# The two score tiles of an attention head in one PSUM bank

## The chip, the core and the metric

The kernel runs on one core of a Trainium2 chip. A core has a matrix engine (TensorE, PE in the rows; its weight loads are PEld), a vector engine (VectorE, DVE), a scalar engine (ScalarE, ACT), GpSimd (POOL) and SyncE (SP), which issues most of the DMAs. Each engine works through its own instructions in the order of the program and waits on semaphores for the others. Matrix products land in PSUM, which has eight banks of 512 float32 values in each of 128 partitions; VectorE and ScalarE read them from there. The metric is the device time of one launch, in microseconds (us), as the median of a few runs.

## The reference

One layer of a streaming encoder, in float32, for 256 prompt rows and 32 rows of a running stream (288 columns in the kernel, which keeps everything transposed): a SwiGLU block, a mixing block with two branches (causal pooling, and latent attention with 16 heads), an output projection, a second SwiGLU block and a last RMSNorm. What matters here is the attention of the prompt rows. With `CHUNK = 64` and blocks of 128 queries it is, for each head:

```python
s = (jnp.einsum('bqhd,bshd->bhqs', qn, k_nope)
     + jnp.einsum('bqhr,bsr->bhqs', qr, k_rope)).astype(jnp.float32) * SM_SCALE
mask = k_chunk[None, :] <= (qp // CHUNK)[:, None]
s = jnp.where(mask[None, None], s, NEG_INF)
p = jax.nn.softmax(s, axis=-1).astype(v.dtype)
return jnp.einsum('bhqs,bshd->bqhd', p, v)
```

The mask lets queries 0 to 63 see 64 keys, 64 to 127 see 128, 128 to 191 see 192 and 192 to 255 see all 256.

## The kernel before, in words

**Weights.** All large products run over weight pieces that are read once. SP loads a piece into a raw buffer, ScalarE rounds it to the high part `whi` (line 185), VectorE subtracts to get the low part `wlo` (line 186), and TensorE forms the product in three passes (high by high, low by high, high by low; lines 151 to 153). Lists of steps are written out by the program and run in that order by `run()` (line 88); before a step's own work come the splits for the steps ahead of it, and what a step leaves for VectorE and ScalarE (its "post") is issued one step later (`later`, line 85). In the attention part a split is cut in two pieces of 512 columns. The schedule is manual: the order of the program is the order on every engine.

**PSUM.** Every product goes to a tile from one pool of eight buffers of one bank each (`acc()`, line 65). A buffer is handed out again when the last reader of its tile is done, and TensorE waits for that at the first product into the new tile.

**Attention.** The loop over heads (line 759) issues for head `hd`: the transposes of the probabilities of head `hd - 1` (`transposes`, line 632), the scores and the softmax of head `hd` (`scores`, line 618), after every fourth head the scores of the running stream for four heads together (`scores4`, line 657), the projections of the next pair of heads as filling work (`fill`, line 751: `q_rope`, `q_nope`, `k_nope`, `values`), the attended values of head `hd - 1` (`attend`, line 641, whose result leaves PSUM at lines 650 and 651), and now and then `spread4` (line 686), which takes the running stream's result of four heads out of one tile, 32 columns at a time, by ScalarE at line 691 and VectorE at line 692.

**Scores of a head.** Two tiles are taken from the pool. `outs[0]` holds queries 0 to 127 by keys 0 to 127 and is made with two float32 products (lines 620, 621). `outs[1]` holds queries 128 to 255 by keys 0 to 255 and is made with five products of split operands (lines 623 to 627). Then `softmax` (line 599) cuts each tile in its upper and lower 64 rows, which gives four pieces with 64, 128, 192 and 256 keys. It issues, in this order: four maxima on VectorE (line 610), four exponentials with a running sum on ScalarE (line 612), one reciprocal on VectorE (line 613) and two scalings of the probabilities on VectorE (line 615). The four maxima of a head stand ahead of its four exponentials in the program. The lines around them:

```python
for _, s, m, _ in seen:
    dve.tensor_reduce(out=m, in_=s, axis=AX.X, op=ALU.max, negate=True)
for p, s, m, t in seen:
    act.activation(p, s, AF.Exp, bias=m, accum_out=t)
```

The functions that the change touches, with the line numbers of the profile:

Of the kernel before, what the change touches and what calls it, by code (L numbers as in the profile page):

```python
# [14 lines left out]
P = 128  # L15
# [30 lines left out]
def kernel(ctx: ExitStack, tc: tile.TileContext, i, o):  # L46
# [18 lines left out]
    def acc():  # L65
        return psa.tile([P, 512], F32, tag="acc", name="acc")
# [532 lines left out]
    def softmax(parts):  # L599

        n = len(parts)
        nb = sm.tile([P, 2], F32, tag="nb", name="nb")
        su = sm.tile([P, 2], F32, tag="su", name="su")
        rs = sm.tile([P, 2], F32, tag="rs", name="rs")
        seen = []
        for b, (p, s, low, high) in enumerate(parts):
            rows = ((0, P, low),) if low == high else ((0, 64, low), (64, P, high))
            seen += [(p[r0:r1, :nk], s[r0:r1, :nk], nb[r0:r1, b : b + 1], su[r0:r1, b : b + 1]) for r0, r1, nk in rows]
# [4 lines that stand above are left out]
        dve.reciprocal(rs[:, :n], su[:, :n])  # L613
        for b, (p, _, _, _) in enumerate(parts):
            dve.tensor_scalar_mul(out=p, in0=p, scalar1=rs[:, b : b + 1])


    def scores(hd):
        outs = (acc()[:, :P], acc()[:, : 2 * P])
        pe.matmul(outs[0], qn[hd][:, :P], kn[hd][:, :P], start=True, stop=False)  # L620
        pe.matmul(outs[0], qr[hd // 2][:, :P], krz[hd % 2][:, :P], start=False, stop=True)
        q, k, r = qns.pop(hd), kns.pop(hd), qrs[hd // 2]
        pe.matmul(outs[1], q[:, 0, :], k[:, 0, :], start=True, stop=False)
        pe.matmul(outs[1], q[:, 0, :], k[:, 1, :], start=False, stop=False)
        pe.matmul(outs[1], q[:, 1, :], k[:, 0, :], start=False, stop=False)
        pe.matmul(outs[1], r[:, hd % 2, :], krh, start=False, stop=False)
        pe.matmul(outs[1], r[:, hd % 2, :], krl[hd % 2], start=False, stop=True)
        p = prompt_p[hd % 2]
        softmax([(p[b], outs[b], b * P + 64, b * P + P) for b in range(2)])
        pr[hd] = p  # L630
# [128 lines left out]
    for hd in range(HEADS + 1):  # L759
        old, four = hd - 1, hd and hd % 4 == 0  # L760
        if hd:
            step(lambda old=old: transposes(old))
        if four:
            step(transposes4)
        if hd < HEADS:
            step(lambda hd=hd: scores(hd))
            if hd % 4 == 3:
                step(lambda hd=hd: scores4(hd // 4))
            fill(hd, 0)
            if hd > 4 and hd % 4 == 1:  # L770
                step(lambda hd=hd: spread4(hd // 4 - 1))
        else:
            wo_parts((3, 0, 0), (3, 0, 1))
        if hd:
            step(lambda old=old: attend(old))
        if four:
            step(lambda old=old: attend4(old // 4))
        if hd < HEADS:
            fill(hd, 1)
        else:  # L780
            wo_parts((0, 1, 0))
            step(lambda old=old: spread4(old // 4))
# [143 lines left out]
```

## Time and profile before

| | |
|---|---|
| median of three runs | 2449.61 us (2449.33 to 2449.8) |
| profiled execution | 2448.82 us, its span 2447.1 us |
| TensorE, products | busy 2423.5 us, 99% of the span |
| TensorE, weight loads | busy 2415.1 us, 99% |
| VectorE | busy 1384.3 us, 57% |
| ScalarE | busy 993.2 us, 41% |
| GpSimd | busy 55.7 us, 2% |
| share of 16 DMA engines | 50.8% in the main queue |

All times in rows are us from the start of the span; a mean is in ns. A busy TensorE is not TensorE at its peak, since products overlap in it and their ends are modelled. The idle time of an engine is put down to the instruction that released it; where two instructions on one engine overlap in the rows, no idle time is shown between them. A number after an x is a count of instructions, and a row of a timeline with x2 or x4 stands for as many instructions in succession, with the name and shape of the first. Attention takes the stretch from about 1217 to 1400 us; the softmax of the first head starts at 1236.8 us.

### The profile page before, as it was taken

How to read it: one execution, taken by the hardware profiler on the slowest of the kernel's cores; microseconds unless marked ns; L12 is line 12 of the kernel's file. 1: busy time of each engine (PE TensorE's matmuls, PEld its weight loads, DVE VectorE, ACT ScalarE, POOL GpSimd, SP SyncE). 2: the span in 40 equal slices, each digit the busy share in tenths (PEclk: the TensorE clock that was granted, in tenths of full speed). 3: DMA queues.
4: the chain of work that ended last, by engine and by line, in shares of the span. 5: the costliest groups of instructions: out<-in, count | busy, mean ns of one | idle time of the engine just before them, and what ended most of it. 6: DMA issues, size and time to landing. Idle time of an engine off the chain costs nothing.

```text
span 2447.1 us, 43880 instructions
## 1 busy us (share of the span) xinstructions
PE 2423.5 (99%) x18298; PEld 2415.1 (99%) x18298; DVE 1384.3 (57%) x2056; ACT 993.2 (41%) x1472; POOL 55.7 (2%) x94
## 2 busy tenths in 40 slices
PE   9999999999999999999999999999999999999998
PEld 9999999999999999999999999999999999999997
DVE  7555555555555776544466675655555555555555
ACT  6333333333333535433367633433333333333334
POOL 0000000000000150000000000000000000000000
PEclk9999999999999999999999999999999999999999
DMA  7556446545644745544422365554554464455444
GB/s 236 174 148 187 164 147 181 173 162 148 189 162 149 221 154 171 185 164 164 155 97 86 113 197 181 162 168 162 148 186 164 147 189 164 158 153 189 164 143 129
DMA packets 129014, 399.71 MB, mean 163 GB/s; under 512 B 16160, under 2 KB 21536, under 8 KB 128816
## 3 DMA queue, kind: packets, MB, share of 16 engines
q1 hardware_dynamic: 126592, 392.73, 50.8%
q8 instruction: 143, 2.34, 0.4%
q0 software_dynamic: 1504, 3.15, 0.4%
q10 hardware_dynamic: 720, 1.04, 0.1%
q14 instruction: 55, 0.45, 0.1%
HBM read 391.35 MB, written 5.51 MB: 162 GB/s over the span
## 4 chain that ended last, share of the span: by engine, by line
PE 60%; issue 35%; ACT 3%; DVE 2%; DMA 0%; POOLq 0%; POOL 0%; ACTq 0%; DVEq 0%
PE acc L152 20%; PE acc L153 20%; PE acc L151 20%; ACT p L612 1%; ACT whi L185 1%; DVE wlo L186 1%; ACT sw L433 0%; DVE nb L610 0%; DVE y L822 0%; ACT kn L564 0%; ACT qrs L185 0%; DVE qn L550 0%; PE acc L225 0%; DVE kns L186 0%; DVE qr L436 0%
## 5 line engine op out<-in xcount | busy, mean ns | idle before, releaser
L186 DVE TENSOR_TENSOR wlo<-raw,whi 128x1024 fp32r<-128x1024 f32 (+2 forms) x858 | 919.4, 1075 | 667.7 <-ACT whi L185 664.0
L185 ACT CAST whi<-raw 128x1024 fp32r<-128x1024 f32 (+2 forms) x858 | 789.7, 925 | 918.4 <-PE acc L152 755.2
L151 PE MATMUL acc<-xh,whi 128*128 128x288 f32 x3600 | 1062.5, 295 | 5.4 <-ACT whi L185 5.4
L152 PE MATMUL acc<-xl,whi 128*128 128x288 f32 x3600 | 1064.1, 296 | 0.0
L153 PE MATMUL acc<-xh,wlo 128*128 128x288 f32 x3600 | 1062.8, 295 | 0.0
L151 PEld LDWEIGHTS acc<-xh,whi 128*128 128x128 f32 x3600 | 678.0, 188 | 5.4 <-ACT whi L185 5.4
L152 PEld LDWEIGHTS acc<-xl,whi 128*128 128x128 f32 x3600 | 678.3, 188 | 0.0
L153 PEld LDWEIGHTS acc<-xh,wlo 128*128 128x128 f32 x3600 | 677.6, 188 | 0.2 <-DVE wlo L186 0.2
L153 PE MATMUL acc<-mh,wlo 128*128 128x288 f32 x1408 | 415.0, 295 | 0.0
L152 PE MATMUL acc<-ml,whi 128*128 128x288 f32 x1408 | 415.0, 295 | 0.0
L151 PE MATMUL acc<-mh,whi 128*128 128x288 f32 x1408 | 414.3, 294 | 0.0
L152 PEld LDWEIGHTS acc<-ml,whi 128*128 128x128 f32 x1408 | 264.7, 188 | 0.0
L151 PEld LDWEIGHTS acc<-mh,whi 128*128 128x128 f32 x1408 | 264.6, 188 | 0.0
L153 PEld LDWEIGHTS acc<-mh,wlo 128*128 128x128 f32 x1408 | 264.6, 188 | 0.0
L277 ACT ACTIVATE s<-z 128x288 f32<-128x288 f32 x88 | 39.0, 445 | 233.4 <-DVE z L275 233.4
L275 DVE TENSOR_TENSOR z<-acc,r 128x288 f32<-128x288 f32 x88 | 40.2, 458 | 88.8 <-PE acc L153 84.7
L281 DVE TENSOR_TENSOR u<-acc,r 128x288 f32<-128x288 f32 x88 | 40.2, 457 | 84.8 <-PE acc L153 84.8
L151 PE MATMUL acc<-oh,whi 128*128 128x288 f32 x256 | 76.1, 297 | 0.5 <-DVE ol L692 0.5
L151 PE MATMUL acc<-mgh,whi 128*128 128x288 f32 x256 | 75.6, 295 | 0.0
L152 PE MATMUL acc<-mgl,whi 128*128 128x288 f32 x256 | 75.5, 295 | 0.0
L152 PE MATMUL acc<-ol,whi 128*128 128x288 f32 x256 | 75.5, 295 | 0.0
L153 PE MATMUL acc<-mgh,wlo 128*128 128x288 f32 x256 | 75.5, 295 | 0.0
(196 smaller groups left out, 1796.5 us busy)
## 6 DMA issues: line engine op xcount, KB each, us to landing
raw<-in_wg SPq DMA_DIRECT2D x172, 512.0 KB, 3.3
raw<-in_wu SPq DMA_DIRECT2D x172, 512.0 KB, 3.3
raw<-in_wd SPq DMA_DIRECT2D x128, 384.0 KB, 3.3
raw<-in_wd SPq DMA_DIRECT2D x128, 320.0 KB, 3.0
raw<-in_wga SPq DMA_DIRECT2D x32, 512.0 KB, 3.3
raw<-in_wgb SPq DMA_DIRECT2D x32, 512.0 KB, 3.3
raw<-in_wo SPq DMA_DIRECT2D x32, 512.0 KB, 3.3
raw<-in_wout SPq DMA_DIRECT2D x32, 512.0 KB, 3.3
```

Of the source, the lines that this page charges most:

```text
L151: pe.matmul(out, hi[:, c], xh, start=first, stop=False)
L152: pe.matmul(out, hi[:, c], xl, start=False, stop=False)
L153: pe.matmul(out, lo[:, c], xh, start=False, stop=last)
L185: act.copy(hi, src)
L186: dve.tensor_tensor(out=lo, in0=src, in1=f(hi), op=ALU.subtract)
L275: dve.tensor_tensor(out=z, in0=ps[:, :T], in1=st["r"], op=ALU.mult)
L277: act.activation(sv[m], z, AF.Silu)
L281: dve.tensor_tensor(out=u, in0=ps[:, :T], in1=st["r"], op=ALU.mult)
L612: act.activation(p, s, AF.Exp, bias=m, accum_out=t)
```

## The change

Instead of one tile for each of the two score blocks, one tile is taken from the pool, and the two blocks are columns 0 to 127 and 128 to 383 of it. A head so takes one PSUM buffer less. The products, the maxima, the exponentials and all shapes stay as they are, and so does their order in the program.

```diff
     def scores(hd):
-        outs = (acc()[:, :P], acc()[:, : 2 * P])
+        both = acc()
+        outs = (both[:, :P], both[:, P : 3 * P])
         pe.matmul(outs[0], qn[hd][:, :P], kn[hd][:, :P], start=True, stop=False)
         pe.matmul(outs[0], qr[hd // 2][:, :P], krz[hd % 2][:, :P], start=False, stop=True)
```

## Rows read from the trace of the kernel before

**Rows 1.** Busy time by stretch: from and to, length, then busy time and count of PE, PEld, DVE, ACT and POOL, the granted TensorE clock (1.00 is full), the DMA share and GB/s. First a stretch of the gate projections ahead of attention, then the stretch from the first softmax to the transposes of head 14.

```profile
1190.00:1210.00 20.00, 20.00 (x154) 20.00 (x152) 9.19 (x10) 7.66 (x11) 0.00 (x0) 1.00 0.48 153
1237.00:1386.40 149.40, 143.19 (x1085) 136.52 (x1083) 101.90 (x280) 106.60 (x328) 0.00 (x0) 1.00 0.28 93
```

**Rows 2.** Who waited for whom between 1225 and 1400 us, PE's own list, its two longest: engine, tile and line that waited, who released it, us in total, times, the longest.

```profile
PE acc L661 <- DVE ol L651: 3.5, 3, 1.4
PE acc L623 <- DVE ol L651: 1.2, 3, 0.4
```

**Rows 3.** The same list for DVE, its two longest and its last; every line left out has ACT as its releaser.

```profile
DVE rs L613 <- ACT p L612: 22.4, 16, 2.5
DVE wlo L186 <- ACT whi L185: 7.3, 17, 2.4
...
DVE nb L610 <- PE acc L621: 0.7, 1, 0.7
```

**Rows 4.** The same list for ACT, whole.

```profile
ACT p L612 <- DVE nb L610: 13.1, 15, 1.3
ACT qns L185 <- DVE qn L550: 12.5, 16, 1.2
ACT qrs L185 <- DVE qr L436: 12.0, 8, 1.5
ACT s L612 <- DVE nb L610: 4.7, 4, 1.2
ACT oh L691 <- DVE ol L692: 3.1, 9, 0.5
ACT pts L639 <- PE acc L637: 1.7, 1, 1.7
ACT vs L591 <- PE acc L583: 1.7, 1, 1.7
ACT L612 <- DVE nb L610: 0.7, 1, 0.7
```

**Rows 5.** All instructions of line 610 in the trace: count, shortest, median and longest in ns, first and last start, and how many of each shape (a head has one of each of the four).

```profile
L610 DVE TENSOR_REDUCE nb<-acc x68: 206/325/428, 1236.8 to 1391.6; 64x1 f32<-64x64 f32 x16, 64x1 f32<-64x128 f32 x16, 64x1 f32<-64x192 f32 x16, 64x1 f32<-64x256 f32 x16
```

**Rows 6.** Timeline of DVE over the softmax of head 7: start, length, engine, line, operation, tiles, shape, count, and the idle time before it with its releaser. The maxima stand in two rows of two, because the answer was cut between the second and the third.

```profile
1312.06 0.51 DVE L610 TENSOR_REDUCE nb<-acc 64x1 f32<-64x64 f32 x2
...
1312.60 0.79 DVE L610 TENSOR_REDUCE nb<-acc 64x1 f32<-64x192 f32 x2
1314.72 0.17 DVE L613 RECIPROCAL rs<-su 128x2 f32<-128x2 f32 x1 [1.32 <-ACT p L612]
```

**Rows 7.** Timeline of ACT over the same softmax: its first exponential and the end of its last one.

```profile
1312.69 0.31 ACT L612 ACTIVATE p<-acc,nb 64x64 f32<-64x64 f32 x1 [1.23 <-DVE nb L610]
...
1314.50 0.19 ACT L612 ACTIVATION_READ_ACCUMULATOR p<-acc,nb 64x1 f32 x1
```

**Rows 8.** The third maximum of the same head in the list by line and shape: busy us, mean ns, idle before.

```profile
L610 DVE TENSOR_REDUCE nb<-acc 64x1 f32<-64x192 f32 x1 | 0.3, 350 | 0.0
```

**Rows 9.** Timeline of ACT in one `spread4`, where ACT and DVE read one PSUM tile in turns, 32 columns each time: the second and the third block.

```profile
1337.98 0.18 ACT L691 CAST oh<-acc 128x32 fp32r<-128x32 f32 x1 [0.52 <-DVE ol L692]
1338.42 0.18 ACT L691 CAST oh<-acc 128x32 fp32r<-128x32 f32 x1 [0.26 <-DVE ol L692]
```

**Rows 10.** Timeline of DVE in the same `spread4`: the first and the second block.

```profile
1337.76 0.18 DVE L692 TENSOR_TENSOR ol<-acc,oh 128x32 fp32r<-128x32 f32 x1
1338.20 0.19 DVE L692 TENSOR_TENSOR ol<-acc,oh 128x32 fp32r<-128x32 f32 x1 [0.25 <-ACT oh L691]
```

**Rows 11.** Timeline of PE in the scores of head 0: the last products into the first and into the second score tile.

```profile
1236.37 0.39 PE L621 MATMUL acc<-krz,qr 128*128 128x128 f32 x2
...
1237.08 0.28 PE L627 MATMUL acc<-krl,qrs 128*128 128x256 f32 x1
```

**Rows 12.** Timeline of DVE in head 0: its four maxima.

```profile
1236.80 1.39 DVE L610 TENSOR_REDUCE nb<-acc 64x1 f32<-64x64 f32 x4 [0.69 <-PE acc L621]
```

**Rows 13.** Timeline of ACT in head 0: the copy of the last value block ahead of it, the load of the exponential's table, and the first exponential.

```profile
1236.35 0.37 ACT L591 COPY vs<-acc 128x256 f32<-128x256 f32 x1 [1.71 <-PE acc L583]
1237.40 1.28 ACT L612 ACT_TABLE_LOAD   x1 [0.68 <-DVE nb L610]
1238.70 0.31 ACT L612 ACTIVATE p<-acc,nb 64x64 f32<-64x64 f32 x1
```

**Rows 14.** Timeline of PE in the scores of head 8: the last product into the second score tile.

```profile
1319.15 0.28 PE L627 MATMUL acc<-krl,qrs 128*128 128x256 f32 x1
```

**Rows 15.** Timeline of DVE in head 8: its first two maxima.

```profile
1319.71 0.51 DVE L610 TENSOR_REDUCE nb<-acc 64x1 f32<-64x64 f32 x2
```

**Rows 16.** Timeline of PE around the transposes of head 14: the last product ahead of them, and the first transpose.

```profile
1385.60 0.29 PE L153 MATMUL acc<-oh,wlo 128*128 128x288 f32 x1
1386.46 0.30 PE L635 MATMUL acc<-ident,p 128*128 128x128 f32 x1 [0.58 <-ACT whi L185]
```

**Rows 17.** Timeline of DVE at the same place: the scalings of the probabilities of head 14.

```profile
1386.03 0.55 DVE L615 TENSOR_SCALAR p<-p,rs 128x128 f32<-128x128 f32 x2
```

**Rows 18.** Timeline of DVE at the end of the softmax of head 15.

```profile
1391.02 0.55 DVE L615 TENSOR_SCALAR p<-p,rs 128x128 f32<-128x128 f32 x2
```

**Rows 19.** Timeline of ACT after the transposes of head 15: the copy of their result.

```profile
1396.50 0.48 ACT L639 COPY pts<-acc 128x384 f32<-128x384 f32 x1 [1.72 <-PE acc L637]
```

**Rows 20.** Timeline of PE at the transposes of head 15.

```profile
1395.92 0.27 PE L635 MATMUL acc<-ident,p 128*128 128x128 f32 x1
```

## The prediction

> **What bounds the kernel now.** The page's first part names TensorE at 99%, and over the whole kernel that is right. The change acts in attention alone, so the view to read next is the busy time by stretch: in the gate projections TensorE is busy for 20.00 of 20.00 us, but from the first softmax to the transposes of head 14 for 143.19 of 149.40 us [rows 1]. There it stands still for 6.2 us, with the clock granted in full.
>
> The list of waits says for what. TensorE's two longest are line 661 (three times, 3.5 us) and line 623 (three times, 1.2 us), both released by VectorE's line 651 [rows 2]. Both are first products into a new PSUM buffer, and line 651 is the last reader of an older one: TensorE has run out of buffers. This is what one buffer less per head bears on.
>
> But a wait for a buffer is a wait for its reader, and the question is what the readers wait for. The lists of VectorE and ScalarE answer it: they wait for each other all through the stage, and for TensorE three times in it, at the first softmax (0.7), at the last value block before that (1.7), and once for 1.7 at line 639, which is after head 15 [rows 3, 4, 13, 19]. So from head 0 on, the chain of VectorE and ScalarE instructions sets the pace, and TensorE is ahead of it by as many buffers as it has. At the end of the stretch the chain catches it: the last product before the transposes of head 14 starts at 1385.60, and the first transpose at 1386.46 after 0.58 us of idleness [rows 16]. The releaser named there is a cast, but the transpose reads the probabilities, whose scalings run from 1386.03 [rows 17]. From that point on TensorE works without a pause worth naming, so what counts is when these scalings are done.
>
> **What the change removes.** Each head takes one buffer less, and TensorE can run further ahead. Counting buffers in the order in which the program frees them, line 661 would then wait for a tile freed long before, and the first product of `k_nope` in an odd head (line 151) would get the one that line 651 frees. The wait moves. I cost this at nothing: readers that never wait for TensorE do not get earlier because TensorE does, and the transposes of head 14 still wait for their probabilities. If that cover were gone, the gain would be bounded by the 6.2 us above (last rival).
>
> **What the change adds: an order between the two engines that read.** In `softmax` four maxima (VectorE) stand ahead of four exponentials (ScalarE), sixteen times in the trace [rows 5]. The exponential needs only its own piece's maximum. Yet in head 7 the first one starts at 1312.69 [rows 7]; the first two maxima run from 1312.06 and are done at 1312.06 + 0.51 = 1312.57, and the other two run from 1312.60 [rows 6]. So it waits for the second maximum, which reads the other 64 rows of the same tile, and not for the third, which reads the other tile. The same shows in `spread4`: ScalarE's second block starts at 1337.98 [rows 9], when VectorE's first block (1337.76 + 0.18 = 1337.94) is done [rows 10], though they read different columns and share only the PSUM tile. Two engines read one tile in turns, in the order of the program, whichever part each of them reads.
>
> With both blocks in one tile, the first exponential therefore waits for all four maxima. These are done at 1312.60 + 0.79 = 1313.39 [rows 6] instead of 1312.57: 0.82 us later. The other three exponentials stand behind it on ScalarE, and behind them the casts and copies of the fillers; on VectorE the reciprocal waits for the last exponential already (1.32 us in this head, 22.4 us in sixteen [rows 3, 6]) and comes 0.82 us later too. Both engines leave the softmax shifted by the same amount. ScalarE has no spare time there that could take it: it waits for the maxima in every head (15 times, 13.1 us, and once at the table load [rows 4]), so it is there early and starts late.
>
> The Trainium skill has the reason in "PSUM — Partial Sum Buffer", section "PSUM bank collisions raise a hardware error": two engines must not touch one bank in the same 32 partitions at once, two reads included. The trace agrees that reads take turns [rows 9, 10]. The page's rule is by 32 partitions, while the first exponential also waits for a maximum of other rows [rows 6, 7]; by the rule alone the wait would be shorter, which is the first rival below.
>
> Lower end for this term: nothing (an ordering that knows columns). Upper end: 0.82 plus another hand-over; from the end of the second maximum to the exponential lie 0.12 us now [rows 6, 7], so 0.94. I take 0.82, since the hand-over is there already.
>
> **The maxima wait for the last product.** VectorE's first maximum now waits for the second block's last product as well. Only head 0 feels this: there VectorE waits for TensorE. The first block is done at 1236.37 + 0.39 = 1236.76 and the second at 1237.08 + 0.28 = 1237.36 [rows 11], so the maxima start 0.60 later. The tightest of the later heads, head 8, has its last product done at 1319.15 + 0.28 = 1319.43 [rows 14] and its first maximum at 1319.71 [rows 15]: 0.28 us to spare, and both of them come later together.
>
> Head 0 in all: maxima from 1237.40 for 1.35 us (1.39 less a wait of 0.04 inside them, an estimate) end at 1238.75. The table load began 0.08 after the second maximum (1237.32, from 1236.80 + 0.51 by head 7's pair) [rows 6, 12, 13]; it would begin at 1238.83 instead of 1237.40. So head 0 adds 1.43 us.
>
> **The sum.** The probabilities of head 14 are later by head 0 and fourteen others: 1.43 + 14 × 0.82 = 12.9 us. TensorE waits for them now, so it is later by the same 12.9. Head 15 adds nothing more: its scalings start at 1391.02 [rows 18], its transposes at 1395.92 [rows 20], and 0.82 fits into that gap of 4.9. The other stages keep their order. The profiled execution took 2448.82, which gives 2461.7; the median of the runs lies 0.79 above the profiled one, and on it the time is 2449.61 + 12.9 = 2462.5.
>
> **Rivals.**
>
> *The order is kept by rows.* The first exponential (rows 0 to 63) waits for the third maximum (same rows) and the second for the fourth. The third takes 0.35 us [rows 8] and ends at 1312.95: 0.38 later than now; the second exponential would be held 0.02 more, since it can't start before 1313.39 + 0.12. Some 0.40 a head, and 1.0 in head 0: 1.0 + 14 × 0.40 = 6.6, so 2456.2. For it: the page's rule. Against it: the first exponential's wait for a maximum of other rows. Chance 0.09.
>
> *No new wait between the readers.* Disjoint columns of one tile are read side by side, so that the change does only what its words say. Then head 0's 0.6 is left: 2450.2. Against it stand the turns in `spread4`. Chance 0.05.
>
> *The freed buffer decides.* TensorE's pauses for buffers go and the stage runs at TensorE's pace: at most 6.2 us of standstill [rows 1] are won, 2443.4. It would take a chain that waits for TensorE somewhere, so that an earlier product makes an earlier reader, and by more than 0.82 us a head. For it speaks that TensorE's longest pauses are for buffers [rows 2]; against it that the readers wait for TensorE nowhere between head 0 and head 14 [rows 3, 4]. Chance 0.04.
>
> *More than the sum.* TensorE's pauses grow from 6.2 to some 19 us in the stretch. At today's pauses of up to 1.4 us the granted clock stays full [rows 1, 2]; should it fall to the lower of its two levels after longer ones, products there would take longer, past 2465. Chance 0.02.
>
> **How the numbers follow.** The forecast as worked out has 0.80. Its own range is 2460 to 2464.5: 0.12 more a head (the upper end above) adds 1.8, and a little slack somewhere takes off as much. The range to hold the time 8 times in 10 also takes in the order by rows, with as much below it: 2455.5 to 2465. What a measurement of this kernel can tell from no change is 0.2%, 4.9 us. Slower by more: the forecast, the order by rows and the last case, 0.91. Within: 0.05. Faster: 0.04.
>
> **What would show it.** In the changed kernel ScalarE's waits for line 610 rise from 13.1 to about 25 us, and VectorE's at line 613 from 22.4 to about 36; the first exponential starts 0.12 after the fourth maximum in every head. The time from the maxima of head 1 to the scalings of head 14 grows by 0.82 a head. TensorE's waits on line 661 go, and others grow: line 151 in odd heads, line 623 for the split keys. Wrong it would be if the first exponential still starts after the second maximum, if the chain waits for TensorE where it doesn't now, or if the shift is there but TensorE doesn't stand waiting at the transposes of head 14.

## The result, and the profile after

The changed kernel takes 2463.07 us (median of six runs, 2462.96 to 2463.6), against 2449.57 (2449.23 to 2449.8) for the kernel before, measured beside it: 13.5 us more. The ratio is 1.0056, with a 95% interval of 1.0045 to 1.0067. The profiled execution took 2463.41 us with a span of 2461.6. The source has one line more inside `scores`, so each number below that is higher by one: 620 is now 621, 651 is 652. In the experiments the numbers shift again with the lines that are put in; the names of the tiles tell what is meant (`nb` a maximum, `p<-acc` an exponential, `acc<-ident,p` a transpose).

The stretch from the first softmax to the transposes of head 14, which answers to [rows 1], has grown from 149.4 to 162.4 us:

```profile
1237.00:1399.40 162.40, 147.09 (x1085) 136.91 (x1083) 102.09 (x280) 107.03 (x328) 0.00 (x0) 1.00 0.26 86
```

The counts of instructions are those of before, and VectorE and ScalarE are busy for the same time within 0.5 us. They have not worked more, they have stood still more. TensorE's busy time has risen by 3.9 us with the same 1085 products. Single products are some 0.3 us long in the rows [rows 14, 16], but 1085 of them took 143.19 us before [rows 1], 0.13 each: they overlap, so that a pause can lie in part under the end of the product ahead of it, and the length of the stretch is the safer number. The granted clock is still 1.00.

Who waited between 1225 and 1412 us, VectorE's list and then ScalarE's (answers to [rows 3, 4]):

```profile
DVE rs L613 <- ACT p L612: 35.9, 16, 3.4
DVE sw L434 <- ACT sw L433: 6.8, 8, 0.9
...
DVE nb L610 <- PE acc L628: 1.3, 1, 1.3
```

```profile
ACT p L612 <- DVE nb L610: 25.2, 15, 2.1
ACT qns L185 <- DVE qn L550: 12.5, 16, 1.2
...
ACT L612 <- DVE nb L610: 2.1, 1, 2.1
ACT vs L591 <- PE acc L583: 1.7, 1, 1.7
ACT pts L640 <- PE acc L638: 0.8, 1, 0.8
```

Two waits have grown by much, both inside the softmax: ScalarE for the maxima from 13.1 to 25.2, VectorE at the reciprocal from 22.4 to 35.9. With them go head 0's two, for the first maximum (0.7 to 1.3) and at the table load (0.7 to 2.1). The others, as `qns`, are within 1.1 us of what they were. The softmax of head 7, VectorE and then ScalarE (answers to [rows 6, 7]):

```profile
1318.46 0.51 DVE L610 TENSOR_REDUCE nb<-acc 64x1 f32<-64x64 f32 x2
...
1318.98 0.79 DVE L610 TENSOR_REDUCE nb<-acc 64x1 f32<-64x192 f32 x2
1321.93 0.17 DVE L613 RECIPROCAL rs<-su 128x2 f32<-128x2 f32 x1 [2.15 <-ACT p L612]
```

```profile
1319.89 0.31 ACT L612 ACTIVATE p<-acc,nb 64x64 f32<-64x64 f32 x1 [2.03 <-DVE nb L610]
```

The four maxima are done at 1318.98 + 0.79 = 1319.77, and the first exponential starts 0.12 us after that. Before, it started 0.12 after the second. The idle times in brackets are longer by 0.80 and 0.83.

All exponentials of line 612 (count; shortest, median and longest in ns; first and last start) and the semaphore waits that stand at that line on ScalarE, first in the kernel before, then in the changed one:

```profile
L612 ACT ACTIVATE p<-acc,nb x64: 308/389/470, 1238.7 to 1390.2; 64x64 f32<-64x64 f32 x16, 64x128 f32<-64x128 f32 x16, 64x192 f32<-64x192 f32 x16, 64x256 f32<-64x256 f32 x16
L612 ACTq EVENT_SEMAPHORE  x32: 17/38/38, 1237.4 to 1389.5; - x32
```

```profile
L612 ACT ACTIVATE p<-acc,nb x64: 310/392/472, 1240.2 to 1404.1; 64x64 f32<-64x64 f32 x16, 64x128 f32<-64x128 f32 x16, 64x192 f32<-64x192 f32 x16, 64x256 f32<-64x256 f32 x16
L612 ACTq EVENT_SEMAPHORE  x16: 17/38/38, 1238.8 to 1402.5; - x16
```

The reads are as long as they were: 389 ns against 392 at the median, and the maxima 325 in both kernels [rows 5]. What has changed is the semaphores, on which one engine waits for another: two waits a head have become one. Before, the second and the fourth maximum of a head raise a semaphore; now only the fourth does. So the order is kept by waits of the program, and no slower read shows.

The last pause of the stage, at the transposes of head 14, TensorE and then VectorE (answers to [rows 16, 17]):

```profile
1399.44 0.30 PE L636 MATMUL acc<-ident,p 128*128 128x128 f32 x1 [1.64 <-ACT whi L185]
```

```profile
1399.01 0.55 DVE L615 TENSOR_SCALAR p<-p,rs 128x128 f32<-128x128 f32 x2
```

Both are later than before by 12.98, and the transposes still start in the middle of the scalings. TensorE's own list of waits, its four longest, shows where it spends the added time:

```profile
PE acc L151 <- DVE ol L652: 4.9, 6, 0.9
PE acc L587 <- ACT whi L185: 2.5, 3, 0.9
PE acc L671 <- DVE s L615: 2.3, 3, 0.8
PE acc L621 <- ACT kn L564: 2.2, 6, 0.4
```

The waits for a buffer at the scores are gone. The same reader (line 652, before 651) is now waited for at line 151.

### The profile page after: what moved, and what is told of

Read it like the earlier page. It is cut to its first block, busy times and chain, and to the rows that moved or that the text cites. A ratio compares the mean times of both kernels' runs of the same rounds, so it can differ in the third digit from the quotient of the medians.

```text
span 2461.6 us, 43860 instructions
## 1 busy us (share of the span) xinstructions
PE 2428.4 (99%) x18298; PEld 2416.5 (98%) x18298; DVE 1384.5 (56%) x2056; ACT 995.8 (40%) x1472; POOL 55.8 (2%) x94
## 4 chain that ended last, share of the span: by engine, by line
PE 59%; issue 35%; ACT 3%; DVE 3%; DMA 0%; POOLq 0%; POOL 0%; ACTq 0%; DVEq 0%
PE acc L152 19%; PE acc L153 19%; PE acc L151 19%; ACT p L612 1%; ACT whi L185 1%; DVE nb L610 1%; DVE wlo L186 1%; ACT sw L433 0%; ACT kn L564 0%; DVE qn L550 0%; DVE y L823 0%; DVE kns L186 0%; PE acc L225 0%; ACT qrs L185 0%; ACT kns L185 0%
## 5 line engine op out<-in xcount | busy, mean ns | idle before, releaser
L151 PE MATMUL acc<-xh,whi 128*128 128x288 f32 x3600 | 1062.3, 295 | 6.0 <-ACT whi L185 6.0
```

The costliest lines, as they stand in the source:

```text
L151: pe.matmul(out, hi[:, c], xh, start=first, stop=False)
```

## The experiments

Three theories were to be told apart. By the first, the wait of the exponentials for all four maxima is the whole cost, passed on by a chain of VectorE and ScalarE that TensorE waits for. By the second, the shared bank itself costs time, or the count of buffers does. By the third, it is the order of issue. Differences are to the median of the kernel before, run on the same chip each time (2448.88 us in the first four runs, 2448.8 in the others).

**The wait without the sharing.** Two tiles as before; only the exponentials are issued backwards.

```diff
-        for p, s, m, t in seen:
+        for p, s, m, t in seen[::-1]:
             act.activation(p, s, AF.Exp, bias=m, accum_out=t)
```

> Two tiles as before, but the four exponentials of a head are issued in the reverse order, so that the first of them reads the second tile and has to wait for the fourth maximum; nothing is shared and no buffer is freed. Theory (the wait of the first exponential for all four maxima is the whole cost): the first exponential starts 0.82 us later in every head, the softmax takes 4.23 us instead of 3.41, head 0 adds 0.87, and the time is 2449.6 + 0.87 + 14 x 0.82 = 2462. Rival (the shared bank itself, or the count of buffers, costs the time): 2449.6, within 1 us.

Measured: 2460.11 us, 11.2 above before (ratio 1.0047, 1.0035 to 1.006). The softmax of head 7, VectorE, ScalarE, and then the transposes of head 14 on TensorE:

```profile
1316.80 1.32 DVE L610 TENSOR_REDUCE nb<-acc 64x1 f32<-64x64 f32 x4
1320.27 0.17 DVE L613 RECIPROCAL rs<-su 128x2 f32<-128x2 f32 x1 [2.15 <-ACT p L612]
```

```profile
1318.24 0.47 ACT L612 ACTIVATE p<-acc,nb 64x256 f32<-64x256 f32 x1 [2.03 <-DVE nb L610]
```

```profile
1397.24 0.30 PE L635 MATMUL acc<-ident,p 128*128 128x128 f32 x1 [1.38 <-DVE p L615]
```

The first exponential again starts 0.12 us after the fourth maximum, with the same idle times as in the changed kernel, though no bank is shared and no buffer is freed. So the wait by itself makes most of the loss. The time is 1.2 us less than expected.

At the transposes of head 14 this kernel is 2.2 us ahead of the changed one (1397.24 against 1399.44), and the traces place this. 0.65 lies in head 0, whose maxima don't wait for the second block here, and 1.54 between the first maxima of head 0 and of head 14. There the last exponential is the shortest, and in head 6 ScalarE's next cast starts 3.34 us after the first maximum (1306.41 against 1303.07) where it takes 3.47 in the changed kernel (1308.04 against 1304.57). The same 0.12 to 0.13 us shows in ten of the eleven heads from 1 to 14 in which a cast comes next, 0.24 in the other. Why the cast starts sooner is not shown. It is not the bank: from the last row of the softmax on ScalarE to that cast it is 0.09 us here, and 0.22 in the changed kernel as it was 0.21 before, with two tiles. The two places make up the 2.2 us.

**The order of issue.** The same instructions by blocks: two maxima, two exponentials, two maxima, two exponentials. Once with the shared tile, once with two.

```diff
-        for _, s, m, _ in seen:
-            dve.tensor_reduce(out=m, in_=s, axis=AX.X, op=ALU.max, negate=True)
-        for p, s, m, t in seen:
-            act.activation(p, s, AF.Exp, bias=m, accum_out=t)
+        for pair in (seen[:2], seen[2:]):
+            for _, s, m, _ in pair:
+                dve.tensor_reduce(out=m, in_=s, axis=AX.X, op=ALU.max, negate=True)
+            for p, s, m, t in pair:
+                act.activation(p, s, AF.Exp, bias=m, accum_out=t)
```

> The changed kernel with another order of the same eight instructions of a head: the two maxima and the two exponentials of the first block, then those of the second. Theory (two engines read one tile in turns, in the order of the program): the first exponential starts 0.63 us after the first maximum again, but now the third maximum waits for the second exponential (some 1.45 us after the first maximum), and the fourth exponential ends where it did; the softmax takes about 4.2 us and the time stays within 1.5 us of the changed kernel, 13 us above before. Rival (the cost comes from the order of issue, which puts all exponentials behind all maxima, and not from the shared tile): the softmax takes 3.4 us and the time falls back to that of before.

> The kernel before with the same order by blocks. Each engine's own list of instructions is the one of before, and the tiles are two. Theory: softmax of 3.41 us, the time of before within 0.5 us. Rival (the order of issue matters by itself): slower by 2 us or more.

Measured: 2464.08 us with one tile, 15.3 above before (1.0062, 1.005 to 1.0075), and 2448.77 with two, which is the time of before (1.000, 0.999 to 1.0009). The one-tile kernel in head 6, VectorE and then ScalarE:

```profile
1304.66 0.51 DVE L611 TENSOR_REDUCE nb<-acc 64x1 f32<-64x64 f32 x2
1306.20 0.79 DVE L611 TENSOR_REDUCE nb<-acc 64x1 f32<-64x192 f32 x2 [1.03 <-ACT p L613]
```

```profile
1305.29 0.31 ACT L613 ACTIVATE p<-acc,nb 64x64 f32<-64x64 f32 x1 [0.73 <-DVE nb L611]
...
1305.71 0.36 ACT L613 ACTIVATE p<-acc,nb 64x128 f32<-64x128 f32 x1
...
1307.08 0.41 ACT L613 ACTIVATE p<-acc,nb 64x192 f32<-64x192 f32 x1 [0.92 <-DVE nb L611]
```

The first exponential starts early, 0.63 us after the first maximum. But the third maximum, which reads other columns than the second exponential, waits until that is done, and the third exponential then waits for the fourth maximum. Reads of one tile take turns in either direction, and the order of issue only says who goes first. From the first maximum to the scalings a head takes 3.75 us here and 3.68 in the changed kernel, and the transposes of head 14 start 0.68 later (1400.12 against 1399.44). The median lies 1.0 us above the changed kernel's, or 1.8 by the differences to before, where 1.5 at most was expected; by the latter count the expectation was missed. With two tiles the same order costs nothing. The third theory falls.

**The freed buffer.** The changed kernel with seven buffers.

```diff
-    psa = ctx.enter_context(tc.tile_pool(name="psa", bufs=8, space=bass.MemoryType.PSUM))
+    psa = ctx.enter_context(tc.tile_pool(name="psa", bufs=7, space=bass.MemoryType.PSUM))
```

> The changed kernel with a pool of seven PSUM buffers instead of eight, which takes back what the change frees. Theory (the chain of VectorE and ScalarE sets the pace in attention, and TensorE's run-ahead is worth nothing): 2463, within 1 us of the changed kernel. Rival (the freed buffer gave a gain that hides part of a larger loss): slower than the changed kernel by 2 us or more, up to the 6 us for which TensorE stood still in the stage before.

Measured: 2463.8 us, 14.9 above before (1.006, 1.0046 to 1.0074), so 1.4 more than the changed kernel has (0.7 by the medians themselves). That is less than the rival's 2 and not clearly within 1, and by itself it decides nothing. The trace says where it comes from. TensorE at the first norm's end, and at the transposes of head 14, with seven buffers, and then at the first of these places in the changed kernel:

```profile
48.03 0.40 PE L151 MATMUL acc<-xh,whi 128*128 128x288 f32 x1 [0.50 <-ACT r L229]
...
1400.43 0.30 PE L636 MATMUL acc<-ident,p 128*128 128x128 f32 x1 [1.38 <-ACT whi L185]
```

```profile
47.38 0.38 PE L151 MATMUL acc<-xh,whi 128*128 128x288 f32 x1
```

In the changed kernel the transposes start at 1399.44. The delay at head 14 is 0.99 us, and 0.65 of it is there at 48 us already, long before attention. The maxima of head 0 start 0.68 later (1238.16 against 1237.48), so the attention stage adds 0.3. The freed buffer is worth next to nothing to it, as the first theory has it.

**The idle time filled.** The exponentials, the reciprocal and the scalings are issued behind the splits of the next weight pieces, two steps after the maxima (three where `scores4` lies between). Once on the changed kernel, once on the kernel before.

```diff
-    def softmax(parts):
+    def softmax(parts, lag):
...
-        for p, s, m, t in seen:
-            act.activation(p, s, AF.Exp, bias=m, accum_out=t)
-        dve.reciprocal(rs[:, :n], su[:, :n])
-        for b, (p, _, _, _) in enumerate(parts):
-            dve.tensor_scalar_mul(out=p, in0=p, scalar1=rs[:, b : b + 1])
+
+        def rest():
+            for p, s, m, t in seen:
+                act.activation(p, s, AF.Exp, bias=m, accum_out=t)
+            dve.reciprocal(rs[:, :n], su[:, :n])
+            for b, (p, _, _, _) in enumerate(parts):
+                dve.tensor_scalar_mul(out=p, in0=p, scalar1=rs[:, b : b + 1])
+
+        later(lag, rest)
...
-        softmax([(p[b], outs[b], b * P + 64, b * P + P) for b in range(2)])
+        softmax([(p[b], outs[b], b * P + 64, b * P + P) for b in range(2)], 3 if hd % 4 == 3 else 2)
...
-        softmax([(pr["new"], out, S - SEQ, S - SEQ)])
+        softmax([(pr["new"], out, S - SEQ, S - SEQ)], 2)
```

> The changed kernel, with the exponentials, the reciprocal and the scalings of a head issued two steps after its maxima, behind the splits of the next weight pieces. ScalarE then casts (1.14 us for two pieces) while it would wait for the maxima (2.05 us), and VectorE subtracts while it would wait for the exponentials. Theory (the cost is idle time of the two readers, which other work can fill): some 1.1 to 1.3 us less a head than the changed kernel, which brings the stage to TensorE's own pace: 2444 to 2448. Rival (two blocks in one bank slow the reads or the products themselves): it stays at 2460 or more.

> The kernel before with the same later exponentials. Theory: the chain gets shorter by about 1.2 us a head and TensorE's 6.2 us of standstill bound the gain: 2443.5 to 2446, and within 2 us of the one-tile kernel with the same order. Rival (the order buys nothing since TensorE sets the pace already): 2449.6.

Measured: 2442.58 us with one tile (0.9974, 0.9964 to 0.9984) and 2441.69 with two (0.997, 0.9958 to 0.9981). Both are faster than expected: 1.4 us below 2444 to 2448, and 1.8 below 2443.5 to 2446. The expectations took TensorE's 6.2 us of standstill as the bound, and the kernel with two tiles won 7.2: the busy time of the stretch holds pauses too, as said above. The two are 0.9 apart, and the intervals of their ratios overlap. The one-tile kernel, head 7 on VectorE and ScalarE, and its stretch from head 0 to the transposes of head 14:

```profile
1309.41 1.67 DVE L610 TENSOR_REDUCE nb<-acc 64x1 f32<-64x64 f32 x5
1311.00 1.28 DVE L186 TENSOR_TENSOR wlo<-raw,whi 128x512 fp32r<-128x512 f32 x2
1312.87 0.17 DVE L615 RECIPROCAL rs<-su 128x2 f32<-128x2 f32 x1 [0.59 <-ACT p L614]
```

```profile
1308.71 1.14 ACT L185 CAST whi<-raw 128x512 fp32r<-128x512 f32 x2
1310.84 0.31 ACT L614 ACTIVATE p<-acc,nb 64x64 f32<-64x64 f32 x1 [0.99 <-DVE nb L610]
```

```profile
1237.00:1379.90 142.90, 140.64 (x1084) 135.90 (x1084) 104.76 (x283) 106.40 (x329) 0.00 (x0) 1.00 0.29 98
```

The exponential still waits for the maxima, but casts fill a part of the time, and subtractions fill most of VectorE's wait for the exponentials (0.59 instead of 2.15). The stretch shrinks from 162.4 to 142.9 us and the sharing, worth 13.5 us in the other order, is worth 0.9. ScalarE's waits for the maxima between 1225 and 1412 us, with one tile and then with two:

```profile
ACT p L614 <- DVE nb L610: 9.2, 12, 1.1
```

```profile
ACT p L614 <- DVE nb L610: 1.4, 7, 0.3
```

So the wait that the sharing adds is still there, but it no longer sets the time. TensorE, which stood still for 15.3 us in the changed kernel's stretch, does so for 2.3 in this one: the stage goes nearly at its pace. That is why this pair alone would not rule out a slower read; the lengths of the reads, shown with the result, do. The second theory falls by them, by the reversed exponentials and by the seven buffers. In the two-tile kernel TensorE has one pause left:

```profile
1377.93 0.30 PE L639 MATMUL acc<-ident,p 128*128 128x128 f32 x1 [1.35 <-DVE p L617]
```

**Head 0 alone.** The changed kernel with a small exponential of ones in the first value step, so that the table of the exponential is loaded there.

```diff
             act.copy(vt[pair][:, 0, :], ps[:, :256])
+            if pair == 0:
+                warm = sm.tile([P, 2], F32, tag="warm", name="warm")
+                act.activation(warm, ones[:, 0:2], AF.Exp)
```

> The changed kernel with one small exponential of ones issued in the first value step, so that the table load of 1.28 us falls where ScalarE waits for TensorE, ahead of head 0. Theory (head 0's delay goes through to the end one to one, since the chain sets the pace from there on): 1.3 us less than the changed kernel, so 12.2 us above before. Rival (head 0's delay is absorbed later by TensorE's lead): no change, 13.5 above before.

Measured: 2461.28 us, 12.5 above before (1.0052, 1.0039 to 1.0064), 1.0 less than the changed kernel's 13.5; the intervals of the two ratios overlap, so the traces have to decide. ScalarE around the load and in head 0, and then TensorE at head 14:

```profile
1232.80 1.28 ACT L600 ACT_TABLE_LOAD   x1
...
1238.80 0.31 ACT L615 ACTIVATE p<-acc,nb 64x64 f32<-64x64 f32 x1 [2.21 <-DVE nb L613]
```

```profile
1397.88 0.30 PE L639 MATMUL acc<-ident,p 128*128 128x128 f32 x1 [1.63 <-ACT whi L185]
```

The first exponential of head 0 starts 1.38 us earlier (1238.80 against 1240.18), and the transposes of head 14 start 1.56 earlier (1397.88 against 1399.44). What is gained at head 0 arrives 160 us later undiminished: nothing in between absorbs it.

**The best version.** Two tiles, the exponentials behind the next casts but one step later only in head 14, and the table loaded early (the two diffs above together, with the lag `1 if hd == 14 else 3 if hd % 4 == 3 else 2`).

> The kernel before with the exponentials behind the next casts, as in the earlier run, but one step later only in head 14, and with the table load ahead of head 0. Theory: TensorE's last pause of that run, 1.5 us at the transposes of head 14, goes, so 1 to 1.5 us less than that run, 8 to 9 us below before. Rival (the pause comes from somewhere else, or TensorE is at its pace already): no change from that run, 7.2 below before.

Measured: 2440.4 us (2439.02 to 2440.76), 8.4 below before; ratio 0.9964, 0.9952 to 0.9977. The stretch, and TensorE at the transposes of head 14:

```profile
1237.00:1375.60 138.60, 138.60 (x1079) 135.13 (x1077) 102.71 (x280) 104.61 (x326) 0.00 (x0) 1.00 0.31 102
```

```profile
1375.64 0.30 PE L642 MATMUL acc<-ident,p 128*128 128x128 f32 x1
```

TensorE is busy in all of the stretch and waits for nothing there. This beats both kernels, with the two tiles of before. The run has two changes over the earlier one, the lag in head 14 and the early table, and does not say what each is worth.

## Why the prediction was right

**What paces the stage.** The step that carried everything was that VectorE and ScalarE wait for each other and not for TensorE. The early table and the seven buffers show it from both sides: 1.4 us taken from the chain at head 0 arrive at head 14, and a buffer taken from TensorE costs 0.3 us in the stage. One bound was too low. The prediction read the 6.2 us of standstill as the most that a faster stage could give, and the casts issued first gave 7.2 with two tiles, the best version 8.4. This bears on a rival alone and not on the sum.

**The order between the readers.** The forecast of 0.82 us a head was right: the first exponential moved from the second maximum to the fourth, with the same 0.12 us between. In the lists of waits, ScalarE's was forecast at about 25 (25.2) and VectorE's at about 36 (35.9).

The rival by rows is out: the first exponential reads rows 0 to 63 and waits for the fourth maximum, which reads rows 64 to 127. The order in this program is by tile; a tile of this pool is a bank, and no run tells the two apart. The rule by 32 partitions in the Trainium skill ("PSUM — Partial Sum Buffer", section "PSUM bank collisions raise a hardware error") would have allowed the shorter wait. Whether the chip would bear these reads side by side was not tried, since taking the wait away would leave the accesses unordered.

**Head 0.** Forecast 1.43, measured 1240.18 - 1238.70 [rows 13] = 1.48. VectorE, then ScalarE:

```profile
1237.48 1.33 DVE L610 TENSOR_REDUCE nb<-acc 64x1 f32<-64x64 f32 x4 [1.28 <-PE acc L628]
```

```profile
1238.89 1.28 ACT L612 ACT_TABLE_LOAD   x1 [2.08 <-DVE nb L610]
1240.18 0.31 ACT L612 ACTIVATE p<-acc,nb 64x64 f32<-64x64 f32 x1
```

**The sum.** 12.9 us were forecast at the transposes of head 14, and 12.98 came; 1.48 and fourteen times 0.82 make 12.96. The time is 13.5 above before instead of 12.9, so about half a microsecond more came in elsewhere. It lies after head 14, where the kernels don't differ: from those transposes to the end of the span it is 1060.6 us in the profile of before, 1062.2 in the changed kernel, 1062.3 with the reversed exponentials, 1061.6 with the early table and 1060.9 with one tile and the casts first. Of the 1.5 us between the first two, 1.1 come from the executions that were profiled: they lie 14.6 apart, the medians 13.5. No new wait shows in that rest. TensorE is busy in all of 1000 us from 1400 before and from 1413 in the changed kernel, and has 7561 products there and 7553. So the rest varies by more than a microsecond from kernel to kernel, for a reason that no run here isolates, and the sum took it as fixed.

**Where TensorE waits now.** That the wait for a buffer would move from line 661 to line 151 was right (six times, 4.9 us). The wait for the split keys, forecast at line 623 (now 624), did not grow: TensorE stops before it, for the unsplit keys at line 621, and it also waits for casts of the value weights at line 587 and for the stream's probabilities at line 671, of which the prediction said nothing. This did not change the time, which follows the shift of the probabilities.

**The other rivals.** That no wait is added is out by the trace after; that the freed buffer decides, by the seven buffers; that the clock falls, by a granted clock of 1.00 in the stretch.

## What to carry to other kernels

Before two results share a PSUM tile, ask which engines read them. In this program two engines that read different parts of one tile take turns, so look in the trace for a pair that does so already, and see whose maximum or copy the other waits for. Before you remove a wait for a buffer, see whether its reader waits for TensorE somewhere: here it did not, and the buffer was worth 0.3 us. If the readers wait for each other, issue other work for both where they meet. Putting the next casts between the maxima and the exponentials was worth 7 us on the kernel before.

## What was not expected

The cost of the sharing all but vanished once other work filled the idle time: 0.9 us instead of 13.5, although the first exponential still waited for the fourth maximum, and ScalarE for the maxima 9.2 us against 1.4. The 0.82 us a head is not a property of the shared bank. It was paid where the two readers set the pace, and hardly at all where TensorE did.

With the shortest exponential last, ScalarE's next cast starts some 0.13 us sooner after the first maximum of its head; why is open.
